# The order of weight slices in the input projection of a hybrid decoder layer: two visits start earlier, the seventh group's first two are re-cut, and a short visit's successor has its first piece traced ahead

## The chip, the cores and the metric

The kernel runs on one core of one Trainium2 chip. The metric is the device time of one execution in microseconds (us), lower is better. Times of a kernel are given as the median of its runs with the lowest and the highest. All data are float32.

## What is computed

One decoder layer and a final norm, for one sequence of 256 tokens with D = 2048 channels. Cut to what matters:

```
mod = silu(c) W_ada + b_ada -> shift1, scale1, gate1, shift2, scale2, gate2
h   = RMSNorm(x) (1 + scale1) + shift1
p   = h W_in      columns: [retention q,k,v,g | HGRN2 q,f,i,g | branch gate A | branch gate B]
yA  = W_retO( LN_head(Retention_chunkwise(rope(q), rope(k), v)) * silu(g) )
yB  = W_hgO( RMS_head(HGRN2_chunkwise(silu(q), f, i)) * silu(g) )
x   = x + gate1 * ( (sigmoid(gA) yA + sigmoid(gB) yB) W_out )
h2  = RMSNorm(x) (1 + scale2) + shift2
x   = x + gate2 * ( conv FFN of h2 )
out = RMSNorm_final(x)
```

The part of interest is the product h W_in together with the modulation that makes h, and the HGRN2 branch that is begun while that product still runs. In HGRN2 the state decays by f per token, f = lb + (1 − lb) sigmoid(hf); within a chunk of 128 tokens the pairs of tokens are weighted by exp of differences of a running sum of log f.

## The kernel before

**Weights.** Each float32 product is made of three products of halves: weight and activation are cut into a high part (fp32r) and a remainder, and hi·hi, hi·lo and lo·hi are added. A weight piece of 1 or 2 slices (a slice is 128 rows of W_in by 512 columns) is loaded raw by a DMA that SP issues (`load`, L161, 11 buffers), ScalarE casts it to the high part `wh` (`upper`, L176), VectorE subtracts to get the remainder `wl` (`rest`, L181), four buffers each. A piece of two slices is 128x1024 in the profile, of one slice 128x512. `pieces` is a generator that hands such pieces on. TensorE then multiplies: `mm_rows` (L205, L206, L210) for groups whose result lies by token, `mm_cols` (L221, L222, L225) for groups whose result lies by channel, `mm_wide` (L255, L258) for the rope groups. Tokens are `act(k)`, the slice k of h (tiles `hT`).

**The first stage.** Twelve groups of 512 columns (the list ATT: two each of HGRN f, q and i, four of gates, two of retention v) times 16 slices k of h. Here groups are counted from 1 in words: the first group is g = 0 in the code, the seventh g = 6, "group 11" g = 10. The slices of h come one after the other, since their scale and shift need W_ada: `ada1(k)` loads four half-megabyte rows, VectorE takes their dot products with silu(c) (L507), ScalarE makes scale and shift of them (L518, L519, L524) and the modulated slice: its high part (L434) and its full value (L435), and VectorE the remainder (L436). These steps are background work: the main loop traces products, and after each piece `pump` lets background generators advance by as many steps as a pace (`pace`) allows. HGRN and retention steps are background generators too (queue 0; W_ada is queue 1).

**Visits.** Because h is not there at once, the groups are *visited*. The generator `visits` goes round the groups, from the fifth on; a visit to a group multiplies the m slices of h that have become available since the last visit. How many are there at a given amount of work (slices multiplied so far) comes from the list READY, in the kernel before (14, 24, 34, 45, 56, ...). The first four groups have had two slices before the visits begin. Groups 1 and 2 keep their PSUM banks; all others use one of two rotating banks `pg`, which `take` empties at the end of each visit: the first time by a copy on ScalarE (L880), later by an addition on VectorE (L882) into the group's sum `p`. `early` traces load, cast and subtraction of the next visit's first piece; in the kernel before this comes after the products of the visit, ahead of `take`. The first pieces of the sixth and seventh groups are loaded ahead with two slices each (`stock`). The plan before has 54 visits.

**What follows.** When the three HGRN groups of a half (f, q, i) are complete, `hgrn` is started as background: sigmoid (L617) and the decay (L622, L625, L628), square root and logarithm, running sums (L636), then levels of a triangle of tokens: a difference on VectorE (L681), exponentials on ScalarE (L684, L685), two multiplications on VectorE (L687, L688), matmuls (L699, L704), masked copies on VectorE (L608); a last level ends with L737 on VectorE ahead of the matmuls L744; then the output matmuls (L763, L765), squares on ScalarE (L769), a root (L353) and a reciprocal (L354), and the scaling on VectorE (L773). Meanwhile four *wide groups* (rope q and k) run in the main loop, each 16 slices into two `pg` banks, which a copy on ScalarE (L276) and an addition on VectorE (L277) empty. `gate_cols` (L531) makes the residual's gate from more W_ada rows, its dots again on VectorE (L507). Later stages are the branch gates, the output projections, the FFN.

**Order.** A scheduler puts the traced instructions into each engine's queue. Outside of pinned stretches it may move them, and each engine works through its queue in order. So where in the program something is traced decides what it stands behind.

Of the kernel before, what the change touches and what calls it, by code (L numbers as in the profile page):

```python
# [23 lines left out]
KT = D // P  # L24
# [8 lines left out]
FIRST = 4  # L33
RESIDENT = 2
ADA_EVERY = 11
READY = (14, 24, 34, *range(45, 156, 11))
NOSYNC = mybir.DependencyInfo(mybir.DependencyClass.NoSync, mybir.DependencyReason.DATA)
SMALL = 70
COLS = (8, 8)
# [21 lines left out]
class Kernel:  # L61
# [784 lines left out]
    def run(self):  # L846
# [29 lines left out]
        def take(g, ps, fresh):  # L876
            for at, z in self.parts(ps, ATT[g] in ROWS):
                dst = accs[g][:, at, :]
                if fresh:
                    nc.scalar.activation(dst, z, AF.Copy)  # L880
                else:
                    nc.vector.tensor_tensor(dst, dst, z, ALU.add)  # L882
# [10 lines left out]
        def opening(k):  # L893

            z = self.s1([P, T], name="z")
            self.pin(nc.scalar.activation(z, self.xT[0][:, k, :], AF.Identity, bias=self.dots[:, 0:1], scale=s1[:, k : k + 1]))
            return z
# [10 lines left out]
        z = opening(0)  # L908
# [26 lines left out]
        z = opening(1)  # L935
# [13 lines left out]
        begun = list(self.pieces(a["wa"][FIRST][:, 0:2, :], 2))  # L949
# [13 lines left out]
        def visit(g):  # L963
            return COLS if g in cols else (0, 0)
# [3 lines left out]
        def begin(kind, hb, *ins):  # L968
            att.append(self.start(kind(hb, *ins, gates)))

        def visits():
            work, g = sum(done), FIRST
            seen = list(done)
            while min(seen) < KT:
                have = 2 + sum(work >= at for at in READY)
                m = have - seen[g]
                if m > 0:
                    yield g, m, work
                    seen[g] = have
                    work += m  # L980
                else:
                    work += 0.5
                g = (g + 1) % len(ATT)
                if have == KT and seen[0] < KT:
                    g = min(i for i in range(len(ATT)) if seen[i] < KT)

        def early(g, m):
            k = done[g]
            pieces = self.pieces(a["wa"][g][:, k : k + m, :], m, shift=visit(g), raw=stock.pop(g, None))
            return chain([next(pieces)], pieces)  # L990

        small = False
        plan = list(visits())
        for g in range(RESIDENT, FIRST):
            take(g, ps[g], True)
        for n, (g, m, work) in enumerate(plan):
            if work > SMALL and not small:
                small = True
                self.small_loads(nc.sync, ("freq", "lbT", "lmask"))
                self.start(self.trig())  # L1000
                self.start(self.lower_bound())
            fresh = done[g] == 0
            have = done[g] + m
            self.finish(*ada[:have])
            bank = ps[g] if g < RESIDENT else self.pg()
            whole = g >= RESIDENT
            self.products(mms[g], bank, a["wa"][g], act, done[g], m, first=whole, last=whole or have == KT, shift=visit(g), begun=begun)
            done[g] = have
            begun = early(*plan[n + 1][:2]) if n + 1 < len(plan) else None
            if whole or have == KT:  # L1010
                take(g, bank, fresh or not whole)
            if have == KT and ATT[g] in GATES:
                nc.scalar.activation(accs[g], accs[g], AF.Silu)
                gates[GATES.index(ATT[g])] = accs[g]
            for hb in range(2):
                gs = [hb, 2 + hb, 4 + hb]
                if g in gs and min(done[i] for i in gs) == KT:
                    self.pace(0, 14.0, 24)
                    begin(self.hgrn, hb, *(accs[i] for i in gs))
                    for i in gs:  # L1020
                        accs[i] = None
# [63 lines left out]
        for j in range(4):  # L1085
            last = j == 3
            x1.append(self.load_rows(j))
            if not last:
                g = self.row(self.gate["gate1"], j, "g1")
            if j == 2:  # L1090
                g3 = self.row(self.gate["gate1"], 3, "g1")
            elif last:
                g = g3
            ps = self.products(self.mm_rows, self.po2() if last else self.pg(), a["wout"][j], actm, 0, KT, hold=4 * last, gain=g if last else None)
            if last:
                g = None
# [14 lines left out]
        begun = [next(up), next(up)]  # L1111
# [287 lines left out]
```

## Time and profile before

| | |
|---|---|
| median of 3 runs | 1512.08 us (1510.61 to 1512.22) |
| profiled execution, own time | 1513.45 us |
| its span | 1511.7 us |
| TensorE busy | 1489.2 us |
| VectorE busy | 1209.0 us |
| ScalarE busy | 836.8 us |

The profile is of one execution. The span runs from its first to its last instruction; the execution's own time is a little longer. A row of the timeline gives the start, the duration, the engine, the line, the operation and its tiles; in brackets stands how long the engine had been idle, and whose semaphore came last. A window row gives the busy time of each engine in a stretch, the clock that TensorE was granted in it (1.00 is full speed), the DMA engines' share and the bytes moved per second.

### The profile page before, as it was taken

How to read it: one execution, taken by the hardware profiler on the slowest of the kernel's cores; microseconds unless marked ns; L12 is line 12 of the kernel's file. 1: busy time of each engine (PE TensorE's matmuls, PEld its weight loads, DVE VectorE, ACT ScalarE, POOL GpSimd, SP SyncE). 2: the span in 40 equal slices, each digit the busy share in tenths (PEclk: the TensorE clock that was granted, in tenths of full speed). 3: DMA queues.
4: the chain of work that ended last, by engine and by line, in shares of the span. 5: the costliest groups of instructions: out<-in, count | busy, mean ns of one | idle time of the engine just before them, and what ended most of it. 6: DMA issues, size and time to landing. Idle time of an engine off the chain costs nothing.

```text
span 1511.7 us, 22801 instructions
## 1 busy us (share of the span) xinstructions
PE 1489.2 (99%) x8537; PEld 1278.6 (85%) x8537; DVE 1209.0 (80%) x1651; ACT 836.8 (55%) x1207; POOL 4.0 (0%) x8
## 2 busy tenths in 40 slices
PE   9999999998999999999999999999999999999997
PEld 8788898887878888888888888888888888888886
DVE  7799997899899977888877787778777769455694
ACT  5655555866775664445456555555555558344342
POOL 0000000000000000000000000000000000000000
PEclk9999999999999999999999999999999999999999
DMA  9999997788688879989947777777777767667561
GB/s 372 329 337 333 333 332 259 233 287 280 216 268 295 295 259 333 318 292 344 338 133 233 245 228 242 238 233 234 233 243 230 228 195 201 197 206 213 179 188 56
DMA packets 111311, 385.73 MB, mean 255 GB/s; under 512 B 12848, under 2 KB 13408, under 8 KB 111200
## 3 DMA queue, kind: packets, MB, share of 16 engines
q1 hardware_dynamic: 110304, 383.14, 76.8%
q8 instruction: 67, 1.10, 0.3%
q10 hardware_dynamic: 896, 1.13, 0.2%
q14 instruction: 44, 0.36, 0.1%
HBM read 382.11 MB, written 2.11 MB: 254 GB/s over the span
## 4 chain that ended last, share of the span: by engine, by line
PE 93%; DVE 3%; ACT 1%; DMA 1%; issue 1%; DVEq 0%; ACTq 0%
PE pg L205 13%; PE pg L210 13%; PE pg L206 13%; PE po L1232 11%; PE pg L1232 10%; PE po L1234 5%; PE pg L1234 5%; PE pg L255 4%; PE po L210 3%; PE po L205 3%; PE po L206 3%; PE pg L258 2%; DVE raw L507 1%; DVE wl L181 1%; DMA raw<-in_wa 1%
## 5 line engine op out<-in xcount | busy, mean ns | idle before, releaser
L181 DVE TENSOR_TENSOR wl<-raw,wh 128x1024 fp32r<-128x1024 f32 (+1 forms) x534 | 633.5, 1194 | 229.5 <-ACT wh L176 215.1
L176 ACT ACTIVATE wh<-raw 128x1024 fp32r<-128x1024 f32 (+1 forms) x534 | 546.1, 1034 | 471.0 <-PE pg L206 192.2
L507 DVE SCALAR_TENSOR_TENSOR raw<-raw,sc 128x1024 f32<-128x1024 f32 (+2 forms) x194 | 234.4, 1212 | 0.0
L205 PE MATMUL pg<-wh,hT 128*128 128x512 f32 x512 | 203.3, 397 | 4.3 <-ACT wh L176 3.0
L206 PE MATMUL pg<-wh,hT 128*128 128x512 f32 x512 | 200.1, 391 | 0.0
L1232 PE MATMUL po<-h2T,wh 128*128 128x512 f32 x704 | 175.8, 392 | 0.0
L1232 PE MATMUL pg<-h2T,wh 128*128 128x512 f32 x688 | 172.2, 393 | 0.0
L1232 PEld LDWEIGHTS po<-h2T,wh 128*128 128x128 f32 x704 | 125.8, 188 | 21.6
L1232 PEld LDWEIGHTS pg<-h2T,wh 128*128 128x128 f32 x688 | 123.0, 188 | 21.1
L210 PE MATMUL pg<-wl,hT 128*128 128x512 f32 x512 | 139.3, 392 | 0.0
L205 PEld LDWEIGHTS pg<-wh,hT 128*128 128x128 f32 x512 | 96.5, 188 | 25.7 <-ACT wh L176 3.7
L210 PEld LDWEIGHTS pg<-wl,hT 128*128 128x128 f32 x512 | 96.7, 189 | 20.5
L206 PEld LDWEIGHTS pg<-wh,hT 128*128 128x128 f32 x512 | 96.5, 189 | 19.3
L1234 PEld LDWEIGHTS po<-h2T,wl 128*128 128x128 f32 x704 | 93.4, 188 | 7.5
L1234 PEld LDWEIGHTS pg<-h2T,wl 128*128 128x128 f32 x688 | 91.4, 188 | 7.3
L1234 PE MATMUL po<-h2T,wl 128*128 128x256 f32 x704 | 94.6, 277 | 0.0
L1234 PE MATMUL pg<-h2T,wl 128*128 128x256 f32 x688 | 92.5, 277 | 0.0
L255 PE MATMUL pg<-hT,wh 128*128 128x512 f32 x256 | 66.0, 401 | 4.7 <-DVE p L277 4.7
L206 PE MATMUL pg<-wh,gs 128*128 128x512 f32 x176 | 68.6, 390 | 0.0
L205 PE MATMUL pg<-wh,gs 128*128 128x512 f32 x176 | 68.6, 390 | 0.0
L205 PE MATMUL po<-wh,gs 128*128 128x512 f32 x176 | 68.6, 390 | 0.0
L206 PE MATMUL po<-wh,gs 128*128 128x512 f32 x176 | 68.5, 389 | 0.0
(271 smaller groups left out, 2021.1 us busy)
## 6 DMA issues: line engine op xcount, KB each, us to landing
raw<-in_wup SPq DMA_DIRECT2D x176, 512.0 KB, 4.6
raw<-in_wdown SPq DMA_DIRECT2D x88, 512.0 KB, 4.1
raw<-in_wa SPq DMA_DIRECT2D x80, 512.0 KB, 5.4
raw<-in_ada SPq DMA_DIRECT2D x64, 512.0 KB, 5.5
raw<-in_wab SPq DMA_DIRECT2D x64, 512.0 KB, 5.4
raw<-in_ada SPq DMA_DIRECT2D x62, 512.5 KB, 5.6
raw<-in_gate SPq DMA_DIRECT2D x32, 512.5 KB, 5.2
raw<-in_wk SPq DMA_DIRECT2D x32, 512.0 KB, 4.6
```

The costliest lines, as they stand in the source:

```text
L176: self.pin(self.nc.scalar.activation(wh, raw, AF.Copy))
L181: self.last = self.nc.vector.tensor_tensor(wl, raw, wh.bitcast(F32), ALU.subtract)
L205: nc.tensor.matmul(ps[t], lhsT=act[:, hi], rhs=wh, start=first and i == 0, stop=False)
L206: nc.tensor.matmul(ps[t], lhsT=act[:, lo], rhs=wh, start=False, stop=False)
L210: nc.tensor.matmul(ps[t], lhsT=act[:, hi], rhs=wl, start=False, stop=last and i == len(items) - 1)
L255: nc.tensor.matmul(ps[z], lhsT=wh[:, z * P : (z + 1) * P], rhs=act, start=first and i == 0, stop=False)
L258: nc.tensor.matmul(ps[z][:, :T], lhsT=wl[:, z * P : (z + 1) * P], rhs=act[:, :T], start=False, stop=last and i == len(items) - 1)
L507: dot = self.pin(nc.vector.scalar_tensor_tensor(raw[:, 0, :], raw[:, 0, :], 1.0, self.sc[:, at:to], ALU.mult, ALU.mult, accum_out=part[:, ...
L1232: self.pin(nc.tensor.matmul(ps[z], lhsT=wh[:, z * P : (z + 1) * P], rhs=act, start=kt == 0, stop=False, skip_group_check=bool(begun)))
L1234: nc.tensor.matmul(ps[z][:, :T], lhsT=wl[:, z * P : (z + 1) * P], rhs=act[:, :T], start=False, stop=kt == KT - 1, skip_group_check=bool(be ...
```

## The change

Three things are edited in the first stage.

1. The list READY is replaced by a formula with LAG = 1: `have = min(KT, 2 + int((work - LAG) / ADA_EVERY))`. With ADA_EVERY = 11 a new slice counts as available at a work of 12, 23, 34, 45, ...; before at 14, 24, 34, 45, .... So only the first two thresholds differ.
2. After the plan is made, the seventh group's first visit gets one slice less, and its second one more. With the new thresholds its first visit would take three slices; now it takes the two that are loaded ahead.
3. For visits of one or two slices, the first piece of the next visit is traced ahead of the visit's products, not behind them.

```
-READY = (14, 24, 34, *range(45, 156, 11))
+LAG = 1
...
-                have = 2 + sum(work >= at for at in READY)
+                have = min(KT, 2 + int((work - LAG) / ADA_EVERY))
...
         plan = list(visits())
+        z = [n for n, (g, _, _) in enumerate(plan) if g == FIRST + 2]
+        for n, m in zip(z, (-1, 1)):
+            plan[n] = (plan[n][0], plan[n][1] + m, plan[n][2])
...
             whole = g >= RESIDENT
+            ahead = early(*plan[n + 1][:2]) if m <= 2 and n + 1 < len(plan) else None
             self.products(mms[g], bank, a["wa"][g], act, done[g], m, first=whole, last=whole or have == KT, shift=visit(g), begun=begun)
             done[g] = have
-            begun = early(*plan[n + 1][:2]) if n + 1 < len(plan) else None
+            begun = ahead or (early(*plan[n + 1][:2]) if n + 1 < len(plan) else None)
```

The new plan has 53 visits instead of 54. The first visits are the same, until group 11's: it now takes four slices instead of three. The slice k = 3 is first needed after 18 slices of visits instead of 21, k = 4 after 27 instead of 28, k = 5 after 40 instead of 41; all later ones as before. At the end the rounds fall differently, and the first HGRN half is started two slices earlier. The number of matmuls is the same; one bank addition (L882) is gone, and two half-width pieces are joined to one.

On ScalarE, at the first visits of groups 10 to 12. Rows read: line, operation, output, input, shape; `pg` is a PSUM bank, `raw` a loaded weight piece. Before:

```order
L880 ACTIVATE p_178<-pg_543 128x1024
L176 ACTIVATE wh_599<-raw_597 128x512
L524 ACTIVATE t_166<-dot_108_558 128x1
L434 ACTIVATE hT_467<-xT_113,t_166,s_165 128x256
L176 ACTIVATE wh_611<-raw_609 128x1024
L435 ACTIVATE h_617<-xT_113,t_166,s_165 128x256
L880 ACTIVATE p_179<-pg_581 128x1024
```

After:

```order
L880 ACTIVATE p_178<-pg_543 128x1024
L524 ACTIVATE t_166<-dot_108_558 128x1
L434 ACTIVATE hT_467<-xT_113,t_166,s_165 128x256
L435 ACTIVATE h_585<-xT_113,t_166,s_165 128x256
L176 ACTIVATE wh_609<-raw_607 128x1024
L176 ACTIVATE wh_630<-raw_628 128x1024
L880 ACTIVATE p_179<-pg_589 128x1024
```

The half-width cast of group 11's third slice is gone, its second piece is a full one, and both halves of the slice's activations stand ahead of that piece's cast.

On TensorE, between the last HGRN output matmul and the fourth wide group, whose banks are `pg_3836` and `pg_3837` before and `pg_3832` and `pg_3833` after. Before:

```order
L255 MATMUL pg_3509<-hT_2290,wh_3749 128x512 x4
L258 MATMUL pg_3509<-hT_1978,wl_3744 128x256 x4
L258 MATMUL pg_3509<-hT_2290,wl_3750 128x256 x4
L763 MATMUL po_3809<-p_173,at_3115 128x128
L765 MATMUL po_3809<-p_173,a_481_3167 128x128
...
L255 MATMUL pg_3836<-hT_230,wh_3840 128x512 x4
```

After:

```order
L765 MATMUL po_3752<-p_173,a_470_3105 128x128
L255 MATMUL pg_3541<-hT_1954,wh_3776 128x512 x4
L255 MATMUL pg_3541<-hT_2288,wh_3782 128x512 x4
L258 MATMUL pg_3541<-hT_1954,wl_3777 128x256 x4
L258 MATMUL pg_3541<-hT_2288,wl_3783 128x256 x4
L255 MATMUL pg_3542<-hT_1954,wh_3776 128x512 x4
L255 MATMUL pg_3542<-hT_2288,wh_3782 128x512 x4
L258 MATMUL pg_3542<-hT_1954,wl_3777 128x256 x4
L258 MATMUL pg_3542<-hT_2288,wl_3783 128x256 x4
L255 MATMUL pg_3832<-hT_230,wh_3836 128x512 x4
```

Before, the L763 and L765 pairs were the last rows ahead of the fourth wide group; now 32 matmuls of the third stand between.

On ScalarE at the same place, where L276 empties the third wide group's banks (`pg_3508` and `pg_3509` before, `pg_3541` and `pg_3542` after). Before:

```order
L769 ACTIVATE sqh_3819,ssh_3818<-po_3809 128x128 x3
L531 ACTIVATE gate_2933<-dot_567_3890 128x1
L769 ACTIVATE sqh_3819,ssh_3818<-po_3809 128x128
L276 ACTIVATE p_3831<-pg_3508 128x512
L353 ACTIVATE rsh_3824<-ssh_3818,eps_73 128x4
L276 ACTIVATE p_3831<-pg_3509 128x512
L617 ACT_TABLE_LOAD
L617 ACTIVATE f_3869<-p_170 128x1024
```

After:

```order
L769 ACTIVATE sqh_3762,ssh_3761<-po_3752 128x128 x4
L531 ACTIVATE gate_2927<-dot_551_3803 128x1
L353 ACTIVATE rsh_3767<-ssh_3761,eps_73 128x4
L617 ACT_TABLE_LOAD
L617 ACTIVATE f_3807<-p_170 128x1024
L276 ACTIVATE p_3827<-pg_3541 128x512
L622 ACTIVATE f_3807<-f_3807,lb,lb_1709 128x256
L276 ACTIVATE p_3827<-pg_3542 128x512
```

The second HGRN half's table load and sigmoid now stand ahead of both copies; before, behind both.

## The prediction

> **What bounds the kernel now.** I read the page's first part, then the waits of TensorE, then the windows around each wait, then the timelines of the engines that stand in front of it.
>
> ```profile
> span 1511.7 us, 22801 instructions
> PE 1489.2 (99%) x8537; PEld 1278.6 (85%) x8537; DVE 1209.0 (80%) x1651; ACT 836.8 (55%) x1207; POOL 4.0 (0%) x8
> ```
>
> TensorE is busy for 1489.2 of 1511.7 us. Both kernels run the same number of matmuls, so a change of order can only move the 22.5 us in which TensorE is idle, and what its clock loses behind an idle stretch. The part of the program whose rows move ends at about 530 us. Its waits are few (25 to 130 us, then 130 to 560 us; the columns are total, count and mean in us):
>
> ```profile
> PE pg L205 <- ACT wh L176: 3.0, 2, 2.1
> ...
> PE po L221 <- ACT wh L176: 1.1, 1, 1.1
> PE pg L222 <- DVE hT L436: 0.4, 1, 0.4
> PE pg L205 <- ACT hT L434: 0.2, 1, 0.2
> ...
> PE pg L255 <- DVE p L277: 4.7, 1, 4.7
> PE pg L205 <- DVE p L882: 1.1, 2, 0.6
> ```
>
> These are 10.5 us, and 4.7 of them are one wait. The larger of the two in the first row is this one, in the timeline of TensorE (start, duration, engine, line, operation; the idle time before it and its releaser in brackets):
>
> ```profile
> 42.48 0.50 PE L205 MATMUL pg<-wh,hT 128*128 128x512 f32 x1 [2.06 <-ACT wh L176]
> ```
>
> The windows (start and end, length, then busy time of PE, PEld, DVE, ACT and POOL, the granted clock, DMA share, GB/s) show where they lie and what follows them:
>
> ```profile
> 43.00:50.00 7.00, 7.00 (x25) 5.54 (x25) 5.05 (x8) 3.34 (x6) 0.00 (x0) 0.76 0.97 347
> 105.00:110.00 5.00, 3.81 (x16) 2.60 (x15) 5.00 (x8) 3.39 (x6) 0.00 (x0) 1.00 0.96 322
> ...
> 368.00:375.00 7.00, 2.26 (x18) 2.01 (x17) 6.38 (x15) 6.89 (x19) 0.95 (x1) 0.99 1.02 409
> 375.00:378.00 3.00, 3.00 (x10) 2.43 (x9) 0.79 (x2) 2.96 (x6) 0.95 (x1) 0.50 0.46 183
> 400.00:450.00 50.00, 50.00 (x568) 40.28 (x567) 50.00 (x66) 37.06 (x52) 0.00 (x0) 1.00 0.77 254
> ```
>
> TensorE runs only 2.26 us between 368 and 375 us, and the next 3 us run at half clock. VectorE is full in two of the rows (5.00 of 5, 50.00 of 50): where TensorE's work is pulled forward past VectorE's, TensorE will wait.
>
> **The change part by part.**
>
> *The first short visits.* The edit that gives this change its name, the first piece traced ahead of the products, moves no row at the first short visits: ScalarE's rows to number 54, VectorE's to 57, SP's to about 40 and TensorE's to about 149 are the same, and the cast of group 8's first piece still stands behind the emptying of a bank. The wait of 2.06 us at 40 us, and the 0.76 clock behind it, therefore stay. Cost: nothing, in either direction.
>
> *(a) The 4.7 us wait.* The timelines of TensorE, ScalarE and VectorE around it:
>
> ```profile
> 364.76 2.09 PE L255 MATMUL pg<-hT,wh 128*128 128x512 f32 x8
> 366.69 1.10 PE L258 MATMUL pg<-hT,wl 128*128 128x256 f32 x8
> 367.62 0.38 PE L763 MATMUL po<-p,at 128*128 128x128 f32 x2
> ...
> 374.31 3.25 PE L255 MATMUL pg<-hT,wh 128*128 128x512 f32 x8 [4.74 <-DVE p L277]
> ```
>
> ```profile
> 368.55 1.06 ACT L176 ACTIVATE wh<-raw 128x1024 fp32r<-128x1024 f32 x1
> 369.63 1.28 ACT L353 ACT_TABLE_LOAD   x1
> 370.92 0.30 ACT L353 ACTIVATE rsh<-ssh,eps 128x4 f32<-128x4 f32 x1
> ...
> 372.51 0.20 ACT L769 ACTIVATION_READ_ACCUMULATOR sqh<-po 128x1 f32 x1
> 372.60 0.59 ACT L276 ACTIVATE p<-pg 128x512 f32<-128x512 f32 x1
> ...
> 373.88 1.28 ACT L617 ACT_TABLE_LOAD   x1
> 375.18 1.06 ACT L617 ACTIVATE f<-p 128x1024 f32<-128x1024 f32 x1
> ```
>
> ```profile
> 373.51 0.66 DVE L277 TENSOR_TENSOR p<-p,pg 128x512 f32<-128x512 f32 x1
> ```
>
> Before, the output matmuls of the first HGRN half (L763, L765) are the last thing ahead of the fourth wide group, so ScalarE works off their squares, a table load and a square root, and only then empties the third wide group's bank (L276 at 372.60); VectorE adds it (373.51) and TensorE starts at 374.31. In the new order 32 more matmuls of the third wide group stand between the last L765 and the fourth group: two sets of 8 + 8, each 367.62 − 364.76 = 2.86 us, so 5.7 us. The third group then ends at about 369.3 + 5.7 = 375.0 us. ScalarE's queue is longer too: the next sigmoid's table load and the sigmoid (L617) now stand ahead of L276. Squares end at 372.6; the square root 0.3; load 1.28; sigmoid about 1.0; so L276 begins at 375.2, ends at 375.7, and L277 takes 0.66 more: TensorE starts at about 376.5. The gap is 1.5 instead of 4.7: **−3.2 us**. VectorE's second set of L773, now ahead of L277, and one more gate dot fit before 375.7. Bounds: the gap is 0.2 if the load of 1.28 comes to lie beside other waits (−4.5), and 4.7 if nothing is won.
>
> The table load: row 369.63 begins right where the cast of 368.55 ends (369.61), and the next operation starts 1.29 us later, so a switch costs 1.3 us here. The Trainium skill's page "ScalarE: Activation LUTs", section "What ACT_TABLE_LOAD costs", speaks against this change: it gives 1283 ns of load and about 1380 ns of drain, 2.66 us for each switch. The load agrees with the row, and no drain stands beside it in this trace; by that rule the gap would be some 1.4 us longer, about the second rival below.
>
> *(b) The clock behind it.* After the 4.74 us gap the 3 us from 375 to 378 run at 0.50, which costs 1.5 us. The row at 43 (0.76) follows a gap of 2.06 us. Behind the shorter waits of 105 to 110 (5.00 − 3.81 = 1.19 us idle) the row shows 1.00. A gap of 1.5 is nearer to those, so I take the half clock as gone: **−1.5 us**; 0 is the other end. The Trainium skill's page "TensorE: Matmul & The Clock Gate", section "Part 1: The HAM clock gate", puts the halving behind an idle window of about 3.4 us; that would take it away for 1.5 as for 2.9 us, but the 2.06 us gap of this trace is already followed by 0.76, so the measurement decides and the term doesn't rest on the page.
>
> *(c) Small waits up to 290 us.* 0.4 + 0.2 + (3.0 − 2.06) + 1.1 + 1.1 = 3.7 us. The visits differ by only a few slices: group 11's first visit takes four slices, VectorE reaches the next slice's dots a little earlier, one bank addition (L882) and two half-width subtractions fewer stand in its queue:
>
> ```profile
> L181 DVE TENSOR_TENSOR wl<-raw,wh 128x1024 fp32r<-128x1024 f32 x166 | 201.1, 1225 | 30.6 <-ACT wh L176 25.7 <-DMA raw<-in_wab 1.5 <-ACT gate L531 1.2
> L507 DVE SCALAR_TENSOR_TENSOR raw<-raw,sc 128x1024 f32<-128x1024 f32 x57 | 69.6, 1222 | 0.0
> L882 DVE TENSOR_TENSOR p<-p,pg 128x1024 f32<-128x1024 f32 x38 | 46.2, 1219 | 6.7 <-PE pg L210 4.2 <-PE pg L225 2.1
> L181 DVE TENSOR_TENSOR wl<-raw,wh 128x512 fp32r<-128x512 f32 x30 | 20.3, 688 | 6.0 <-ACT wh L176 3.0 <-PE po L225 2.9
> ```
>
> Freed are 1.22 + 2 × 0.69 = 2.6 us of a full engine, about 70% of the 3.7. But some of these waits end at a cast, not at VectorE. I take half: **−1.85 us**, from 0 to −3.7.
>
> *(d) A new wait at 59 us.* Group 11's second piece now holds the third slice, and its cast goes behind both halves of that slice's activations:
>
> ```profile
> 59.22 0.39 PE L205 MATMUL pg<-wh,hT 128*128 128x512 f32 x1
> ```
>
> ```profile
> 58.14 0.28 ACT L524 ACTIVATE t<-dot 128x1 f32<-128x1 f32 x1
> 58.46 0.60 ACT L434 ACTIVATE hT<-xT,t,s 128x256 fp32r<-128x256 f32 x1
> 58.97 1.04 ACT L176 ACTIVATE wh<-raw 128x1024 fp32r<-128x1024 f32 x1
> ```
>
> A half-width cast goes out ahead of L524 and a half slice of activation (L435) comes in, of about one size, so this cast still begins at 58.97 and ends at 60.0. TensorE wanted its weights at 59.22: **+0.8 us**; 0 if other matmuls of the first piece last longer.
>
> *(e) The HGRN steps pulled forward.* Up to the first L744 TensorE has 32 wide matmuls fewer ahead of it (5.7 us), up to the second 24 512-wide ones (8 take 366.69 − 364.76 = 1.93 us, so 5.8 us). VectorE, which feeds it through L737, has fewer rows ahead by the means above: 1.22 × 3 + 2 × 0.69 = 5.0 us, and for the second 1.22 × 2 + 1.38 = 3.8 us.
>
> ```profile
> 354.84 0.76 PE L744 MATMUL po<-eq,kt 128*32 128x32 f32 x64
> ...
> 447.74 0.76 PE L744 MATMUL po<-eq,kt 128*32 128x32 f32 x64
> ```
>
> ```profile
> 353.30 0.63 DVE L737 TENSOR_TENSOR eq<-e,q 128x256 f32<-128x256 f32 x1
> ...
> 445.27 0.66 DVE L737 TENSOR_TENSOR eq<-e,q 128x256 f32<-128x256 f32 x1
> ```
>
> Slack before: 354.84 − 353.93 = 0.9 and 447.74 − 445.93 = 1.8 us. TensorE comes closer by 0.7 and 2.0: no wait at the first, 0.2 at the second. **+0.2 us**, from 0 up to the third rival's price. From about 530 us on all engines' rows are the same.
>
> **Sum.** −3.2 − 1.5 − 1.85 + 0.8 + 0.2 = −5.55 us. The profiled execution took 1513.45 us (1.75 more than its span), which would become 1507.9; it lies 1.4 above the median of the runs shown, 1512.08. On the median: **1506.5 us**. With (a) to (c) and (e) at their better ends, −4.5 − 1.5 − 3.7 + 0.8 = −8.9: 1503.2.
>
> **The rivals.** A measurement of this kernel can tell about 0.2% (3.0 us) from no change: faster is below 1509.1, slower above 1515.1.
>
> 1. *The boundary stays shut.* ScalarE empties its banks in queue order, and the sigmoid's load and the second L773 set move ahead of L276 and L277; if they are as late against TensorE as the squares were, (a) and (b) are nothing: −1.85 + 0.8 + 0.2 = −0.85, **1511.2**. For it: ScalarE is busy 6.89 of 7 us there. Against: 5.7 us of matmuls come between and only 2.3 us of ScalarE's work.
> 2. *Each table switch costs more than its row.* If the load that now stands ahead of L276 holds ScalarE for twice its 1.28 us, the gap is 2.8: (a) −1.9, and since 2.8 is above the 2.06 that brought 0.76, (b) 0. −1.9 − 1.85 + 0.8 + 0.2 = −2.75, **1509.3**. The rows at 369.63 and 370.92 speak against it. It is the case that the Trainium skill's page "ScalarE: Activation LUTs" would give.
> 3. *VectorE is the real bound (the slower side).* TensorE's HGRN matmuls come forward by 5.7 and 5.8 us, but VectorE is full (50.00 of 50 from 400 to 450) and its steps don't come forward with them. Then TensorE waits 5.7 − 0.9 = 4.8 at the first L744 and 5.8 − 1.8 = 4.0 at the second, and (c) is nothing as well: −3.2 − 1.5 + 0.8 + 8.8 = +4.9, **1517.0**. Each microsecond by which VectorE comes forward takes 2 off it; it is slower than before as long as VectorE comes forward by under 2.4 us, half of what its shorter queue allows, and measurably so under 0.9 (4.9 − 2 × 0.9 = 3.1). Against it: those rows did go from its queue.
> 4. *The change does not do what it says.* The first piece isn't ahead in any queue that matters, and later visits only swap places without touching a wait: **1512.1**.
>
> **How the numbers follow.** The forecast has 0.52: its largest term is one wait with a plain cause, and the matmuls that fill it are in the new order. Its own range is 1503.2 to 1509.1. Rival 1 has 0.23, rival 2 0.05, rival 3 0.15 (0.13 of it above 1515.1), rival 4 0.05. Faster: 0.52. Within 0.2%: 0.23 + 0.05 + 0.02 + 0.05 = 0.35. Slower: 0.13. The range goes from 1503.2 to 1512.5, which takes in rivals 1, 2 and 4 and leaves out most of the third.
>
> **What would show it.** In the profile after: the wait of L255 on L277 near 370 us at 1.5 us instead of 4.74, and a clock of 1.00 behind it (a, b); the two waits near 40 us and their 0.76 as before; the waits at 105, 127 and 283 us summing to half (c); a new wait of under 1 us of L205 on the cast near 59 us (d); no wait above 0.3 us at the L744s (e). A wait over 4 us at the third boundary means rival 1, idle of TensorE on L737 or L688 between 310 and 460 us rival 3. If the time falls by more than 9 us, a term is missing: something that I hold to be unmoved, the rows behind 530 us above all, would have moved in time.

## The result, and the profile after

| | before | after |
|---|---|---|
| median | 1512.15 us (1510.61 to 1513.54, 4 runs) | 1504.28 us (1503.31 to 1506.08, 4 runs) |
| ratio | | 0.9948 (95% interval 0.9932 to 0.9964) |
| profiled execution | 1513.45 us, span 1511.7 | 1506.08 us, span 1504.3 |

The change makes the kernel 7.9 us faster; 5.55 was forecast, and the time lies inside the forecast's range (1503.2 to 1512.5). The page of the profile after, first part:

```profile
span 1504.3 us, 22803 instructions
PE 1489.4 (99%) x8537; PEld 1278.1 (85%) x8537; DVE 1208.0 (80%) x1649; ACT 835.4 (56%) x1206; POOL 4.0 (0%) x8
```

TensorE is busy for the same time as before (1489.4 against 1489.2 us), so the 7.4 us by which the span is shorter show as idle time of TensorE. Its busy time hides two changes of the clock: the half clock near 375 us is gone, and in this execution TensorE ran from 12.6 to 19.4 us at half clock, where the execution before had 1.00 (18 matmuls of L248 take 3.68 us there, before 2.17). That stretch lies ahead of every row that moved and costs little, since TensorE then waits less behind it: by 26.5 us it is only 0.2 us late. What TensorE still waits for, from 25 to 130 us and then from 130 to 560 us (total, count, longest, in us):

```profile
PE pg L205 <- ACT wh L176: 2.7, 2, 2.1
PE po L242 <- DVE hT L887: 0.5, 1, 0.5
```

```profile
PE pg L205 <- DVE p L882: 0.6, 1, 0.6
PE pg L255 <- DVE p L277: 0.3, 1, 0.3
```

The 4.7 us wait of L255 is 0.3 now; of the small waits of the prediction's part (c) only one of 0.6 is left. In the 2.7 of L205 on the cast are the 2.06 us of before and a new wait of 0.65. The windows, in the columns of the prediction:

```profile
43.00:50.00 7.00, 7.00 (x25) 5.58 (x24) 5.23 (x8) 3.37 (x6) 0.00 (x0) 0.76 1.03 409
...
105.00:110.00 5.00, 5.00 (x23) 4.13 (x22) 5.00 (x8) 1.16 (x2) 0.00 (x0) 1.00 0.96 325
...
368.00:375.00 7.00, 6.88 (x38) 6.00 (x39) 4.86 (x8) 6.98 (x10) 0.00 (x0) 1.00 0.50 170
375.00:378.00 3.00, 3.00 (x19) 2.63 (x18) 3.00 (x4) 2.97 (x4) 0.00 (x0) 1.00 0.99 331
400.00:450.00 50.00, 49.93 (x562) 40.24 (x548) 49.01 (x68) 34.98 (x56) 0.00 (x0) 1.00 0.87 287
```

Between 368 and 375 us TensorE now works 6.88 us where it worked 2.26, and no stretch behind it runs at half clock. The 0.76 of 43 to 50 us is as before. The third wide boundary, TensorE and then ScalarE:

```profile
361.88 0.39 PE L765 MATMUL po<-p,a 128*128 128x128 f32 x2
362.02 2.09 PE L255 MATMUL pg<-hT,wh 128*128 128x512 f32 x8
...
366.71 1.09 PE L258 MATMUL pg<-hT,wl 128*128 128x256 f32 x8
368.12 2.12 PE L255 MATMUL pg<-hT,wh 128*128 128x512 f32 x8 [0.31 <-DVE p L277]
```

```profile
355.79 0.30 ACT L531 ACTIVATE gate<-dot 128x1 f32<-128x1 f32 x1 [1.49 <-DVE raw L507]
...
361.07 1.28 ACT L353 ACT_TABLE_LOAD   x1
...
364.51 1.28 ACT L617 ACT_TABLE_LOAD   x1
365.80 1.06 ACT L617 ACTIVATE f<-p 128x1024 f32<-128x1024 f32 x1
366.77 0.58 ACT L276 ACTIVATE p<-pg 128x512 f32<-128x512 f32 x1
```

The 32 matmuls of the third wide group stand behind the last L765, from 362.02 to 367.80, and under them ScalarE does the last four squares (L769), two roots (L353), a table load and the sigmoid (L617). L276 starts 1.0 us before the group ends.

### The profile page after: what moved, and what is told of

The parts are those of the page before. It is cut to its first block, busy times and chain, and to the rows that moved or that the text cites. A ratio compares the mean times of both kernels' runs of the same rounds, so it can differ in the third digit from the quotient of the medians.

```text
span 1504.3 us, 22803 instructions
## 1 busy us (share of the span) xinstructions
PE 1489.4 (99%) x8537; PEld 1278.1 (85%) x8537; DVE 1208.0 (80%) x1649; ACT 835.4 (56%) x1206; POOL 4.0 (0%) x8
## 4 chain that ended last, share of the span: by engine, by line
PE 93%; DVE 3%; ACT 1%; DMA 1%; issue 1%; SPq 0%; DVEq 0%; ACTq 0%
PE pg L205 13%; PE pg L210 13%; PE pg L206 13%; PE po L1236 11%; PE pg L1236 10%; PE po L1238 5%; PE pg L1238 5%; PE pg L255 4%; PE po L206 3%; PE po L210 3%; PE po L205 3%; PE pg L258 2%; DVE wl L181 1%; DVE raw L507 1%; PE pg L225 1%; PE pg L222 1%
## 5 line engine op out<-in xcount | busy, mean ns | idle before, releaser
L181 DVE TENSOR_TENSOR wl<-raw,wh 128x1024 fp32r<-128x1024 f32 (+1 forms) x533 | 631.2, 1194 | 226.2 <-ACT wh L176 217.4
L176 ACT ACTIVATE wh<-raw 128x1024 fp32r<-128x1024 f32 (+1 forms) x533 | 544.9, 1035 | 463.3 <-PE pg L206 189.1
L205 PE MATMUL pg<-wh,hT 128*128 128x512 f32 x512 | 203.2, 397 | 3.4 <-ACT wh L176 2.7
L206 PE MATMUL pg<-wh,hT 128*128 128x512 f32 x512 | 200.4, 391 | 0.0
L205 PEld LDWEIGHTS pg<-wh,hT 128*128 128x128 f32 x512 | 96.4, 188 | 24.9 <-ACT wh L176 3.8
L206 PEld LDWEIGHTS pg<-wh,hT 128*128 128x128 f32 x512 | 96.5, 189 | 19.4
L206 PE MATMUL pg<-wh,gs 128*128 128x512 f32 x176 | 68.6, 390 | 0.0
L205 PE MATMUL pg<-wh,gs 128*128 128x512 f32 x176 | 68.5, 389 | 0.0
L205 PE MATMUL po<-wh,gs 128*128 128x512 f32 x176 | 68.5, 389 | 0.0
L206 PE MATMUL po<-wh,gs 128*128 128x512 f32 x176 | 68.5, 389 | 0.0
L1249 ACT ACTIVATE u<-uy,convw 128x256 f32<-128x256 f32 x88 | 52.3, 595 | 28.7 <-DVE uy L1247 28.4
```

Source lines behind the costliest of these rows:

```text
L176: self.pin(self.nc.scalar.activation(wh, raw, AF.Copy))
L181: self.last = self.nc.vector.tensor_tensor(wl, raw, wh.bitcast(F32), ALU.subtract)
L205: nc.tensor.matmul(ps[t], lhsT=act[:, hi], rhs=wh, start=first and i == 0, stop=False)
L206: nc.tensor.matmul(ps[t], lhsT=act[:, lo], rhs=wh, start=False, stop=False)
L1249: nc.scalar.activation(u, y, AF.Identity, bias=w[3], scale=w[2])
```

## The experiments

**Theory.** Of the gain, about 6 us are one place, the third wide boundary: where the HGRN output matmuls fall against it, and with them the order in ScalarE's queue. It is set by how the plan of visits ends, some 300 us after the edited visits. The rest is small waits that the earlier second threshold shifts. **Rivals.** The tracing ahead earns it; the earlier slices earn it; pulled forward, VectorE takes it back.

**1. Without the tracing ahead.** The changed kernel with

```
-            ahead = early(*plan[n + 1][:2]) if m <= 2 and n + 1 < len(plan) else None
...
-            begun = ahead or (early(*plan[n + 1][:2]) if n + 1 < len(plan) else None)
+            begun = early(*plan[n + 1][:2]) if n + 1 < len(plan) else None
```

> The changed kernel without the edit that traces the next first piece ahead of short visits; thresholds and re-cut stay. Theory (the place): that edit moves no row on any engine, and the gain comes from where the plan puts the HGRN outputs: 1504.3 us within 0.1%, wait at the third wide boundary 0.3 us. Rival (the edit named first earns it): the time goes back most of the way, to 1510 or more.

Measured: 1504.66 us (1504.37 to 1505.73), ratio to the kernel before 0.9949 (0.9936 to 0.9961), as good as the changed kernel's 0.9948. The edit that the change is named after does nothing: in the two traces all rows of TensorE, ScalarE and VectorE stand in the same order, so the scheduler had put the next piece where it is with or without it.

**2. The second threshold alone.** The kernel before with

```
-READY = (14, 24, 34, *range(45, 156, 11))
+READY = (14, 23, 34, *range(45, 156, 11))
```

> The kernel before with only the second threshold changed (24 to 23), so that the rounds at the end of the stage fall as before and no matmul of the third wide group stands behind the last output matmuls. Theory (the place): the 4.7 us wait and the half clock behind it stay; what is gained is only in the small waits of the first 130 us (0.55 at 74, 1.75 at 105, less 0.9 for the new wait at 59): about 1510.5. Rival (the earlier slice earns the gain): the time is that of the changed kernel, 1504.3.

Measured: 1510.71 us (1508.32 to 1512.63), ratio 0.9989 (0.9980 to 0.9997). The waits at 74 and 105 us are gone, the new one at 59 us has come, and at the third boundary TensorE waits 4.75 us as before. The half clock goes from 370.15 to 376.97 us there, twice as long as before (374.90 to 378.31). So the earlier slice is worth about 1.9 of the 7.9 us (0.5 to 3.0 by the interval). The rest comes with the first threshold, by way of a plan of 53 visits that ends otherwise; experiment 3 shows that the re-cut isn't needed for it. The first threshold alone was not run.

**3. Both thresholds, no re-cut, no tracing ahead.** The changed kernel without the lines on `ahead` (as in 1) and without

```
-        z = [n for n, (g, _, _) in enumerate(plan) if g == FIRST + 2]
-        for n, m in zip(z, (-1, 1)):
-            plan[n] = (plan[n][0], plan[n][1] + m, plan[n][2])
```

> Both thresholds changed, without the re-cut of the seventh group's visits and without tracing ahead. Theory (the place): 32 matmuls stand behind the last outputs as in the changed kernel, the wait there is under 0.6 us. At 40 us the seventh group's third slice waits about 0.6 us for its activation's high part and 0.7 us for its remainder, which takes the place of the 2.06 us wait; no wait of over 1.5 us is left and the clock behind it stays at 1.00: 2.5 us less than the changed kernel, 1501.8. Rival (the re-cut is needed): the third slice waits 2 to 3 us and more, with the clock down behind it: 1505 to 1507.

Measured: 1503.43 us (1503.17 to 1504.37), ratio 0.9940 (0.9928 to 0.9953). Its waits of TensorE at 40 us:

```profile
40.01 0.50 PE L205 MATMUL pg<-wh,hT 128*128 128x512 f32 x1 [0.42 <-ACT hT L434]
41.31 0.50 PE L206 MATMUL pg<-wh,hT 128*128 128x512 f32 x1 [0.80 <-DVE hT L436]
```

```profile
43.00:50.00 7.00, 7.00 (x32) 1.00 1.03 412
```

The two short waits are there as expected, in place of the 2.06, and the clock behind them is 1.00 (last columns: busy time of TensorE, clock, DMA share, GB/s). But the waits at 72 and 103 us, which the changed kernel had lost, are back (0.8, 0.4 and 1.2 us; counted from the start of one matmul to the start of the next, over the usual step). So the gain on experiment 1, which ran beside it, is 1.2 us, of the 2.5 expected. The plans of this kernel and the changed one differ only in the seventh group's first two visits (3 and 3 slices here, 2 and 4 there): one slice there moves waits 60 us later. The re-cut trades the 40 us place for those; it is not needed for the gain.

**4. The cast put ahead in fact.** The changed kernel, in which the copy that empties the seventh group's bank and the third slice's shift are ordered behind the cast of group 8's first piece:

```
-        self.pin(self.nc.scalar.activation(wh, raw, AF.Copy))
+        self.cast = self.nc.scalar.activation(wh, raw, AF.Copy)
+        self.pin(self.cast)
...
-        self.pin(act(sh[:, kk], part[:, 0:1], AF.Identity, bias=part[:, 1:2]))
+        ins = self.pin(act(sh[:, kk], part[:, 0:1], AF.Identity, bias=part[:, 1:2]))
+        if name == "ada1" and k == 2:
+            self.tc.add_manual_dep(ins.ins, self.cast.ins.name, NOSYNC, reason="behind the next cast")
...
-                    nc.scalar.activation(dst, z, AF.Copy)
+                    ins = nc.scalar.activation(dst, z, AF.Copy)
+                    if g == FIRST + 2:
+                        self.tc.add_manual_dep(ins.ins, self.cast.ins.name, NOSYNC, reason="behind the next cast")
```

> The changed kernel with the cast of group 8's first piece ordered ahead of the emptying of the seventh group's bank and of the third slice's shift, so that what is traced ahead also stands ahead in ScalarE's queue. Theory: its weights landed at 39.45 us, so the cast runs from 39.5 to 40.6, the 2.06 us wait shrinks to about 0.2 and the 0.76 clock behind it goes (1.7 us): 3.6 us less, 1500.7. Rival (the transfers set the pace there, DMA share 1.03): the wait comes back within 10 us at the next pieces, and the time is 1503 to 1504.3.

Measured: 1501.28 us (1500.98 to 1502.80), ratio 0.9927 (0.9914 to 0.9941): 3.4 us less than experiment 1, which ran beside it. ScalarE, then TensorE, then the window (inserted lines shift the numbers: L883 is the L880 of the changed kernel, L206 its L205):

```profile
38.39 1.05 ACT L176 ACTIVATE wh<-raw 128x1024 fp32r<-128x1024 f32 x1
39.58 1.03 ACT L883 ACTIVATE p<-pg 128x1024 f32<-128x1024 f32 x1
```

```profile
39.49 0.50 PE L206 MATMUL pg<-wh,hT 128*128 128x512 f32 x1
```

```profile
43.00:50.00 7.00, 7.00 (x32) 1.00 1.03 414
```

The cast (L176) runs while TensorE is still at the seventh group, the copy (L883) behind it, and group 8 begins without a wait. This is what the words of the change promise. The earlier line in the program alone does not bring it; the ordering dependence, set on the cast that was traced earlier, does. The transfers were not the limit: from 40 to 50 us TensorE is busy for all 10.00 us.

**5. Only the place of the HGRN outputs.** The kernel before with

```
-        self.pace(0, 143.0, 88)
+        self.pace(0, 155.0, 88)
```

> The kernel before, with one number changed: background work in the wide groups is let forward at 155 instead of 143 us for 88 steps, which puts 32 matmuls of the third wide group behind the last HGRN output matmuls, with ScalarE's order there as in the changed kernel. Visits, thresholds and early waits stay as before. Theory (the place): the 4.7 us wait shrinks to about 0.3 and the half clock goes, -4.4 and -1.5: 1506.5 us against 1512.4. Rival (the gain hangs on the earlier start of the slices and of the HGRN half, not on the place of the output matmuls; pulled forward alone, VectorE is late): waits of 3 us and more at L704 and L744 take it back, 1510 or more.

Measured: 1507.37 us (1505.79 to 1508.33), ratio 0.9964 (0.9952 to 0.9977). Its waits from 130 to 560 us:

```profile
PE pg L205 <- DVE p L882: 1.1, 2, 0.6
PE pg L205 <- DVE p L277: 0.4, 1, 0.4
PE pg L255 <- DVE p L277: 0.3, 1, 0.3
```

About 5.0 us of the 7.9 come from one number that touches none of the visits; the wait of L255 is 0.3 as in the changed kernel. No L744 or L704 waits. The missing 0.9 of the expected 5.9 is in part a new wait of 0.4 behind the fourth wide group; the rest is not explained.

**6. Half the matmuls between.** The changed kernel with 139 in place of 143 in the same line.

> The changed kernel, with background work in the wide groups let forward at 139 instead of 143: 16 matmuls of the third wide group instead of 32 stand behind the last output matmuls, and ScalarE has one square instead of four and the root between the sigmoid and the first copy. Theory: 2.86 us less cover, some 1.5 us less queue: a wait of about 1.7 us at the third boundary. If the clock falls behind it as it did behind 2.06 us (0.76 over 7 us) the time is 1504.4 + 1.4 + 1.7 = 1507.5; if a wait of 1.7 leaves the clock at 1.00, as 1.4 us and less did, 1505.8. Rival (the place does not matter): 1504.4.

Measured: 1504.81 us (1504.61 to 1506.17), ratio 0.9951 (0.9939 to 0.9964). Both numbers of the theory missed, and the time is that of the rival, in which the place does not matter: there is no wait at the third boundary. ScalarE and TensorE there:

```profile
363.80 1.07 ACT L617 ACTIVATE f<-p 128x1024 f32<-128x1024 f32 x1
364.77 0.26 ACT L769 ACTIVATE sqh<-po 128x128 f32<-128x128 f32 x1
...
365.02 0.59 ACT L276 ACTIVATE p<-pg 128x512 f32<-128x512 f32 x1
```

```profile
365.26 1.09 PE L258 MATMUL pg<-hT,wl 128*128 128x256 f32 x8
366.38 2.10 PE L255 MATMUL pg<-hT,wh 128*128 128x512 f32 x8
```

Only one of the second tile's four squares, and not the root behind them, now stands ahead of L276; it starts at 365.0, before the third group's last matmuls (365.26) have begun, and the fourth group follows them at 366.38. A wait of 0.8 us behind the fourth group is new. The trace tells why: from the start of the last L765 to the start of L276 it is now 1.8 us (363.19 to 365.02), in the changed kernel 4.9 (361.88 to 366.77). The edit took 3.1 us from ScalarE's queue, not the 1.5 expected, and 2.9 us of matmuls from TensorE's side, so the two cancel. The wait is the difference of both, and an edit that moves both can't tell which of them matters. Experiment 8 moves ScalarE's order alone.

**7. More work for VectorE.** The changed kernel with the difference at the start of the last level done four times:

```
-        nc.vector.tensor_tensor(e, bb, bb[:, :, :, 1:2].to_broadcast([P, 8, 32, 4]), ALU.subtract)
+        for _ in range(4):
+            nc.vector.tensor_tensor(e, bb, bb[:, :, :, 1:2].to_broadcast([P, 8, 32, 4]), ALU.subtract)
```

> The changed kernel with one subtraction of VectorE, the difference at the start of each HGRN half's last level, done four times instead of once (same result): 3 x 1.14 = 3.4 us more for VectorE in each half. It prices the third rival. If VectorE has no reserve beyond the slack at L744 (347.53 - 346.62 = 0.9 and 434.93 - 434.27 = 0.7), TensorE waits 2.5 and 2.7 us more: 1504.4 + 5.2 = 1509.6. If VectorE catches up in its other work, or is not what L744 waits for, 1504.4 to 1505.5.

Measured: 1513.04 us (1511.78 to 1514.23), ratio 1.0004 (0.9995 to 1.0013): 8.4 us more than experiment 1, and more than the 5.2 of a VectorE without reserve. But nearly all of the wait came elsewhere than at L744 (0.3 us there, 0.6 at the output matmuls of the second half): at the second wide boundary. VectorE, ScalarE and TensorE there (the repeated line is L724, the exponentials L727 and L728):

```profile
341.93 1.22 DVE L724 TENSOR_TENSOR e<-b 128x1024 f32<-128x1024 f32 x1
```

```profile
343.18 0.67 ACT L727 ACTIVATE eq<-e 128x512 f32<-128x512 f32 x1 [1.61 <-DVE e L724]
343.76 0.65 ACT L728 ACTIVATE e<-e 128x512 f32<-128x512 f32 x1
344.43 1.08 ACT L276 ACTIVATE p<-pg 128x512 f32<-128x512 f32 x2
```

```profile
346.18 3.75 PE L255 MATMUL pg<-hT,wh 128*128 128x512 f32 x8 [5.39 <-DVE p L277]
```

The exponentials wait for VectorE, the copies L276 stand behind them, and TensorE waits 5.39 us with half clock behind it (8 matmuls in 3.75 us instead of 2.12). There a bank's copy stands behind a slow chain: it is the same trap as that of the kernel before, at another boundary. It shows that VectorE has no reserve at this place; what a late VectorE costs at L744 alone, as the third rival priced it, it does not settle.

**8. The copies traced earlier, TensorE's order as before.** The kernel before with the emptying moved into the loop of `wide_group`, ahead of `pump`:

```
                 self.mm_wide(ps, items, k == 0, k == steps[-1], pair)
+                if k == steps[-1]:
+                    if pair == 0:
+                        out = self.blk([P, 4, T], name="p")
+                    dst = out[:, pair : pair + 2, :]
+                    z = pgs[pair // 2][2]
+                    nc.scalar.activation(dst, z[:, :, T:], AF.Copy)
+                    nc.vector.tensor_tensor(dst, dst, z[:, :, :T], ALU.add)
                 self.pump()
```

> The kernel before, with the emptying of a wide group's two banks (L276, L277) traced right behind the last matmuls of each bank instead of behind the group. TensorE's rows stay as before, no matmul of the third wide group stands behind the last output matmuls, but the copies now stand ahead of the squares of the second token tile. It tells the place of the output matmuls from the order in ScalarE's queue. Theory, narrowed (the order in ScalarE's queue decides; the matmuls behind the outputs only give it time): the first bank is free before TensorE comes to the fourth group, the second at about 372.4 of the old time, when TensorE wants it: a wait of at most 0.5 us instead of 4.7, no half clock, 1506.5 us. Rival (only matmuls put between the outputs and the fourth group help): the wait stays above 3 us, 1511 or more.

Measured: 1506.97 us (1505.54 to 1508.04), ratio 0.9959 (0.9947 to 0.9972). ScalarE, VectorE and TensorE (L766 is the last output matmul):

```profile
363.00 0.60 ACT L276 ACTIVATE p<-pg 128x512 f32<-128x512 f32 x1 [2.58 <-PE pg L258]
...
369.49 0.58 ACT L276 ACTIVATE p<-pg 128x512 f32<-128x512 f32 x1
```

```profile
364.72 0.72 DVE L277 TENSOR_TENSOR p<-p,pg 128x512 f32<-128x512 f32 x1
...
370.38 0.66 DVE L277 TENSOR_TENSOR p<-p,pg 128x512 f32<-128x512 f32 x1
```

```profile
368.03 0.39 PE L766 MATMUL po<-p,a 128*128 128x128 f32 x2
368.17 2.09 PE L255 MATMUL pg<-hT,wh 128*128 128x512 f32 x8
...
371.10 2.10 PE L255 MATMUL pg<-hT,wh 128*128 128x512 f32 x8
```

The fourth group follows the last output matmul directly, with nothing of the third between: the wait is gone because the first bank is emptied by 365.4 us and the second by 371.04, and TensorE comes to the second at 371.10. TensorE's rows stand in the order of the kernel before. So the order in ScalarE's queue alone can take the wait away, and the rival, in which only matmuls in between help, falls. In the changed kernel it is the other side that does it: its copy starts later behind the last L765 than before (4.9 us against 3.4), and the 5.8 us of matmuls cover it. A wait of 0.8 us behind the fourth group is new here, as in experiment 6.

**9. Both.** Experiment 4 and the edit of experiment 8 on the changed kernel.

> The changed kernel with both: the cast of group 8's first piece ordered ahead (as in the earlier run of that) and the wide groups' banks emptied right behind their matmuls. Theory: at 40 us the gain of the earlier run, 3.4 us; at the wide boundaries only 0.3 to 0.5 us is left to win: 1500.9, not to be told from 1501.3. Rival (copies that move ahead push HGRN's steps back, and VectorE is full): up to 1503.

Measured: 1501.61 us (1501.14 to 1501.87), ratio 0.9924 (0.9911 to 0.9938): as good as experiment 4 (not run beside it), to within what can be told. The wide boundaries have no wait left, and one of 0.7 us has come at the matmuls of an HGRN level (L704). Experiments 4 and 9 are the fastest versions here, 11 us below the kernel before.

## Why the prediction was right, point by point

- **The first short visits**: right. No row moved, the 2.06 us wait and the 0.76 are there; experiment 1 shows that this edit moves no row anywhere in the program.
- **(a)** The mechanism was right, its size too small: 4.74 became 0.31, so −4.4 for −3.2. The step that was off is "Squares end at 372.6": it took ScalarE's queue up to there as it was. Before, a gate row stood between the squares and waited:

```profile
366.51 0.30 ACT L531 ACTIVATE gate<-dot 128x1 f32<-128x1 f32 x1 [1.10 <-DVE raw L507]
```

After, its like waits ahead of the squares (355.79), and the first root's load starts 0.8 us ahead of the last L765 (361.07 and 361.88) where it started 0.4 behind (369.63 and 369.18). That is the 1.2 us. The bound (a gap of 0.2) took in the result, but for another reason: it let the load lie beside a wait, and what moved was the wait of a gate row. That the matmuls in between cover the queue is right for this kernel, and experiment 5, in which they are moved without the visits, bears it out; experiment 8 shows that it was not the only way.
- **(b)** Right: the clock from 368 on is 1.00. The half clock before lasted from 374.90 to 378.31, 3.41 us, so it cost 1.7 rather than the 1.5 of the window.
- **(c)** Too small: 3.7 became 0.6, −3.1 for −1.85. About 0.9 came back in three stalls on L181 too short for the table of waits (at 92, 128 and 131 us; 0.25 to 0.31 each from start to start, over the usual step). The wait at 127 is gone because one cast more stands ahead of a table load there (three in a row from 119.8 us instead of two).
- **(d)** Right in place and nearly in size, 0.65 for 0.8:

```profile
60.19 0.50 PE L205 MATMUL pg<-wh,hT 128*128 128x512 f32 x1 [0.65 <-ACT wh L176]
```

- **(e)** Right at the first L744 and 0.2 too much at the second: there is no wait at either. The rows of the first, VectorE's and TensorE's:

```profile
345.98 0.64 DVE L737 TENSOR_TENSOR eq<-e,q 128x256 f32<-128x256 f32 x1
```

```profile
347.53 0.76 PE L744 MATMUL po<-eq,kt 128*32 128x32 f32 x64
```

The slack is 347.53 − 346.62 = 0.9 us, as before: VectorE came forward by as much as TensorE (7.3 us), where 0.7 less was expected. At the second it fell from 1.8 to 0.7.
- **The sum**: −4.4 − 1.7 − 3.1 + 0.9 + 0.65 = −7.65, and +0.2 from the start of the program, which the change does not touch; the two profiled executions differ by 7.37. The medians differ by 7.9. Of the 2.1 us between 7.65 and the forecast's 5.55, 1.2 are (a); the rest is spread over the other four terms, none above 0.35. Two readings were off without touching the sum: the third column of the table of waits is the longest wait, not the mean, and TensorE's rows are the same only from about 547 us on, not 530.
- **The rivals**: the first (the boundary stays shut) did not happen. Of the fourth the first half is true (the first piece is ahead in no queue, experiment 1), but the later visits did touch waits. The second, in which a table switch holds ScalarE for more than its row, falls by the rows at 364.51 and 365.80: the load takes 1.28 and the sigmoid follows at once. The Trainium skill's "ScalarE: Activation LUTs", section "What ACT_TABLE_LOAD costs", adds about 1.38 us of drain to each load; this trace has none. The third did not happen, though its premise, a VectorE without reserve, holds at the one place where experiment 7 tried it.

## What to carry to other kernels

Tracing an instruction earlier in the program is not the same as having it earlier in a queue: compare the engines' rows, and where none moves, expect nothing; here an ordering dependence did what the earlier line alone did not. Where a bank that the next group needs is emptied by an engine that also serves a slow chain, see what stands ahead of the emptying in that engine's queue: the wait is that queue less the matmuls that cover it, and moving either side was enough here (experiments 5 and 8). A change of a plan's first numbers can pay at its end: look for its gain where the phases meet, not where the numbers stand.

## What the runs showed of the hardware that was not expected

Whether the clock falls behind a wait of 2.06 us depends on how the wait lies in steps of 3.41 us. In seven traces here (before, after and experiments 1, 2, 6, 7 and 8) one such step of half clock follows the wait at 40 us; in experiment 5, with the same wait of 2.06 us at the same place, the clock stayed up. In all eleven traces the changes of the clock within a trace lie whole multiples of 3.413 us apart: before, for one, half clock goes from 43.81 to 47.22 and from 374.90 to 378.31, and 374.90 is 97 such steps behind 43.81. The steps begin at another time in each execution. The windows below, in the columns of the prediction, are cut at these steps. Before:

```profile
40.40:43.81 3.41, 1.35 (x7) 1.09 (x7) 1.35 (x2) 3.35 (x5) 0.00 (x0) 1.00 1.02 402
43.81:47.22 3.41, 3.41 (x10) 2.64 (x9) 3.41 (x6) 1.07 (x2) 0.00 (x0) 0.50 0.95 323
368.08:371.49 3.41, 1.49 (x14) 1.30 (x12) 3.05 (x3) 3.36 (x8) 0.95 (x1) 1.00 1.02 407
371.49:374.90 3.41, 0.59 (x3) 0.53 (x4) 3.23 (x13) 3.35 (x11) 0.00 (x0) 1.00 1.02 407
374.90:378.31 3.41, 3.41 (x12) 2.84 (x11) 0.89 (x3) 3.37 (x6) 0.95 (x1) 0.50 0.44 177
```

Experiment 5 (a half clock that ends at 16.57 us sets the steps, and seven of them later one begins at 40.46, inside the wait):

```profile
37.05:40.46 3.41, 2.86 (x13) 2.05 (x11) 2.29 (x5) 2.40 (x5) 0.00 (x0) 1.00 1.02 400
40.46:43.88 3.42, 1.91 (x8) 1.60 (x9) 1.93 (x3) 3.42 (x6) 0.00 (x0) 1.00 1.04 407
43.88:47.29 3.41, 3.41 (x16) 2.82 (x16) 3.41 (x5) 1.40 (x2) 0.00 (x0) 1.00 0.98 338
```

A step in which TensorE is idle for 2.06 us (busy 1.35) is followed by half clock, a step with 1.92 (busy 1.49) is not; in experiment 5 the wait is cut into 0.55 and 1.51, and neither part is enough. In the seven traces the 2.06 us lie in one step. Once the clock is down, less keeps it down: in experiment 2 a step at half clock with 1.48 us idle (370.15 to 373.56) is followed by another. So the border is between 1.92 and 2.06 idle us of a step in these traces, and a wait of 2 us is a matter of chance, while those of 4.74 and 5.39 us were followed by half clock each time. From 20 us on no wait under 1.5 us was. At the start of the program idle time does not tell it all: in the profile after, the half clock from 12.58 us follows a step with only 0.54 us idle, filled with small matmuls (128x128 at L339, 128x1 at L375); what decides there was not tried. The Trainium skill's "TensorE: Matmul & The Clock Gate", section "What's actually happening", gives a window of 3413 ns and calls it "free-running"; the steps of these traces agree, though no run here varied their position on purpose. One step at half clock costs a busy TensorE 1.7 us, so this kernel's time can move by that much from run to run with the place of one wait.
